# A hybrid decoder block on one core: substitution on 16x16 blocks, two copies of the merged inverses, and state updates through a PSUM bank of their own

## The chip, the cores and the metric

The kernel runs on one core of a Trainium2 chip. The metric is the time of one execution on the device in microseconds (us). Matrix products run on TensorE (PE; its weight loads are listed apart as PEld), elementwise work on VectorE (DVE), ScalarE (ACT) and GpSimd (POOL); DMAs are issued from the queues of SyncE (SP) and of ACT. Each engine takes its instructions in a fixed order and waits on semaphores for the others.

## What is computed

One decoder layer over 2048 tokens of width 1024: an RMS norm, one input projection of 3080 columns that feeds three mixers (a convolution module with 31 taps, a gated DeltaNet with 4 heads of 64, and differential attention with 4 heads), an output projection with the residual, and a SwiGLU feed-forward part of width 2816. All in float32. The change lies in the DeltaNet. Its core, per head and per chunk of c = 64 tokens:

```python
lower = jnp.where(strict, beta[..., None] * kk * decay, 0.0)
a_mat = lower + jnp.eye(c)
sol = lax.linalg.triangular_solve(a_mat, rhs, left_side=True, lower=True, unit_diagonal=True)
u_c, w_c = sol[..., :dv], sol[..., dv:]
def step(state, inp):                       # one chunk after the other
    v_new = u_i - w_i @ state
    o_i = (q_i * exp(g_i)) @ state + qk_i @ v_new
    state = state * exp(g_last) + (k_i * exp(g_last - g_i)).T @ v_new
```

## The kernel before

The 2048 tokens are worked on in four units (u = 0 to 3) of U = 512 tokens, which is 8 chunks of 64. With 4 heads a unit has 32 triangular systems of 64x64. A list of steps sets the order in which the program is written (line 937): for each unit N (first norm, `ln1`), I (`gdn_in`: the DeltaNet's part of the projection, with `gdn_gates`, `gdn_decays` and `gdn_conv`), G (`gdn_unit`), C (`conv_in` and `conv_taps`), L (`conv_ln`), K and V (queries, keys and values of attention). A scheduler then orders the instructions of each engine once, at build time; that order is fixed on the chip. After these steps come the rest of attention and the feed-forward part, from about 1000 us on.

The projection's matmuls are done by `mm3` (lines 137 to 139) in three products of a high and a low half; tiles `mz`, `mq`, `ma`, `mw`, `mg`, `mv` are its results in two PSUM banks that take turns, so a matmul into one waits for the eviction of the one before the last (for `ma` the DVE operation that makes `ql`). In unit 0 each weight tile is split into halves by ACT (line 120) and POOL (line 121, a tensor_tensor on 128x512 in SBUF), and written back to DRAM (`ws`); later units load both halves (`wp<-ws`) through SP's queue.

`gdn_unit` makes the matrix `L` (tokens of a chunk on partitions), writes it to DRAM (`gL`) and reads its two diagonal 32x32 blocks back as `Lg`, one system on each of 64 partitions. Lines 466 to 472 invert them: 31 steps, in each a product `tm` and a subtraction from `Tt`, each on DVE and each waiting for the one before. `Tt` and its transpose go out to `gT` and come back by ACT's DMA queue as `X64` (lines 480 to 482) and `T1` (line 483). Two groups of 32x32 matmuls (`yp` line 490, `wp` line 500, not to be mixed up with the weight tile `wp`) merge the two 32x32 inverses into the 64x64 inverse, and the result is put into `X64`. There is one `X64` for all units. Then the scan goes through the 8 chunks: `vp` (lines 542 and 545), its copy `vn` on ACT, `op` (550, 553), and `dp`, the product that updates the state (557); line 562 adds it to the state `Sbd`, one operation on 64x64 for each head.

`conv_taps` sums 31 taps for two halves of the channels on DVE (lines 586 to 593), with the sum in the PSUM tile `cp` until the last tap writes `ca` in SBUF.

Of the kernel before, what the change touches and what calls it, by code (L numbers as in the profile page):

```python
# [26 lines left out]
H = 4  # L27
# [20 lines left out]
def body(ctx: ExitStack, tc: tile.TileContext, x, norm1_g, w_in, conv_dw_w, conv_dw_b,  # L48
# [17 lines left out]
    gT = [dram.tile([2, 2, H, 8, 32, 32], F32, name=f"gT{u}", tag=f"gT{u}") for u in range(NU)]  # L66
# [6 lines left out]
    def cst(shape, name):  # L73
        return const.tile(shape, F32, name=name, tag=name)
# [115 lines left out]
    ps_ca = p1bctx.enter_context(tc.tile_pool(name="ps_ca", bufs=1, space=PSUM))  # L190
# [57 lines left out]
    X64 = cst([P, H, TU, C], "X64")  # L248
    V.memset(X64, 0.0)
# [8 lines left out]
    def sct_(name):  # L258
        return ps_sc.tile([P, 512], F32, name=name, tag="sc")
# [78 lines left out]
    def sm(u, name, n=16, bufs=1):  # L338
        return gd.tile([P, n], F32, name=f"{name}{u}", tag=name, bufs=bufs)
# [4 lines left out]
    def gdn_gates(u, abt):  # L344
# [12 lines left out]
        for c in (15, 13, 11, 9, 7, 5, 3):  # L357
# [14 lines left out]
        Gc, E1, Ek, EGL = sm(u, "Gc"), sm(u, "E1"), sm(u, "Ek"), sm(u, "EGL", 32, 2)  # L372
# [57 lines left out]
    def gdn_unit(u, qtok, sc):  # L430
        L, QKT = sc["L"], sc["QKT"]
# [25 lines left out]
        nc.scalar.dma_start(gL[u].rearrange("h (t p) c -> p (h t) c", p=P), L.rearrange("p h t c -> p (h t) c"))  # L457

        Lg = gd.tile([64, 32, 32], F32, name=f"Lg{u}", tag="Lg")
        Tt = gd.tile([64, 32, 32], F32, name=f"Tt{u}", tag="Tt")  # L460
        for blk in range(2):
            b0 = blk * 32
            nc.scalar.dma_start(Lg[b0:b0 + 32], gL[u].rearrange("h (c r) s -> (h c) r s", c=8)[:, b0:b0 + 32, b0:b0 + 32])
        V.memset(Tt, 0.0)
        V.memset(Tt.rearrange("p a b -> p (a b)")[:, 0:1024:33], 1.0)
        for j in range(31):
            n = 31 - j
            tm = gd.tile([64, 256], F32, name=f"tm{u}_{j}", tag="tg")
# [7 lines left out]
        T1 = gd.tile([P, H, TU, 32], F32, name=f"T1_{u}", tag="Lg")  # L476
        for ch in range(2):
            for blk in range(2):
                r0 = ch * C + blk * 32
                nc.scalar.dma_start(  # L480
                    X64[r0:r0 + 32, :, :, blk * 32:blk * 32 + 32].rearrange("p h t c -> p (h t) c"),
                    gT[u][1, blk].rearrange("h (t c) s q -> c s (h t) q", c=2)[ch])
            nc.scalar.dma_start(T1[ch * C:ch * C + 32].rearrange("p h t c -> p (h t) c"),
                              gT[u][0, 0].rearrange("h (t c) s q -> c s (h t) q", c=2)[ch])
# [98 lines left out]
    def conv_taps(u, hc):  # L583

        acc2 = gd.tile([P, 2, U], F32, name=f"ca{u}", tag="ca")
        for ct in range(2):
            acc = ps_ca.tile([P, U], F32, name=f"cp{u}_{ct}", tag="cp")
            for j in range(31):
                w, hj = cwT[:, ct, j:j + 1], hc[:, ct, j:j + U]
                if j == 0:  # L590
                    V.tensor_scalar(acc, hj, w, cwT[:, ct, 31:32], op0=ALU.mult, op1=ALU.add)
                else:
                    V.scalar_tensor_tensor(acc2[:, ct, :] if j == 30 else acc, hj, w, acc, op0=ALU.mult, op1=ALU.add)  # L593
        return acc2

    def conv_ln(u, acc2):
# [405 lines left out]
    hx = Rot([P, U], F32, (gd, "Tt"), (gd, "Lg"), (gd, "L"))  # L1002
# [261 lines left out]
```

## Time and profile before

| | us |
|---|---|
| median of 3 executions (2912.79 to 2918.99) | 2916.71 |
| the profiled execution | 2917.14 |
| its span, first to last instruction | 2915.4 |
| PE busy in the span | 2800.1 |
| DVE busy | 1565.9 |
| ACT busy | 1050.0 |
| POOL busy | 1111.3 |

Busy times are of the whole span, and the stages differ: the part before 1000 us holds all of the DeltaNet, the rest is attention and feed-forward. A busy time of PE counts overlapping matmuls once. Where a row names a wait, the number in brackets is the engine's idle time before the instruction, and the name behind the arrow is what ended it.

### The profile page before, as it was taken

Reading aid. Unit: us, or ns where it says so; the run is one execution under the profiler, and the core shown is the slowest. Engines: PE = TensorE matmul, PEld = TensorE weight load, DVE = VectorE, ACT = ScalarE, POOL = GpSimd, SP = SyncE. Lnnn points to the kernel's source line nnn. Section 1 sums busy time; section 2 is a strip of 40 time slices with the busy share of each in tenths; the row PEclk is TensorE's granted clock in tenths of the full one; section 3 lists DMA queues with packets and bytes.
Section 4 is the critical chain, followed back from the end, with each engine's and each line's share of the span. In section 5 each row is a group of like instructions: output and inputs, shape, how many; then the busy total and the mean of one; then the engine's idle time right before and its main releaser. Section 6 shows DMA issues by size and latency. Waiting matters only on the chain.

```text
span 2915.4 us, 39754 instructions
## 1 busy us (share of the span) xinstructions
PE 2800.1 (96%) x14673; PEld 2284.4 (78%) x14673; DVE 1565.9 (54%) x3443; ACT 1050.0 (36%) x2237; POOL 1111.3 (38%) x1021
## 2 busy tenths in 40 slices
PE   7979989999988999999998999999999999999998
PEld 6867777778776788887877888887878888888886
DVE  8976776877766765565566655541332222422223
ACT  4333223322154544444455434442332222322222
POOL 4421010001033444344455434444644444444543
PEclk9989999999988999999999999999999999999999
DMA  7784573654776544444366344324343333323332
GB/s 253 242 274 153 178 232 127 207 179 138 254 200 219 144 131 122 112 126 118 108 182 203 86 130 120 93 88 151 102 149 99 96 94 101 116 87 102 101 94 87
DMA packets 404064, 422.52 MB, mean 145 GB/s; under 512 B 46448, under 2 KB 326170, under 8 KB 392606
## 3 DMA queue, kind: packets, MB, share of 16 engines
q1 hardware_dynamic: 344222, 373.31, 41.8%
q10 hardware_dynamic: 59648, 46.67, 5.1%
q8 instruction: 116, 1.90, 0.3%
q14 instruction: 78, 0.64, 0.1%
HBM read 344.35 MB, written 75.56 MB: 144 GB/s over the span
## 4 chain that ended last, share of the span: by engine, by line
PE 80%; DVE 8%; DMA 6%; issue 2%; ACT 2%; POOL 1%; ACTq 0%; SPq 0%; POOLq 0%; DVEq 0%
PE pg L137 6%; PE pg L138 6%; PE pg L139 6%; PE pu L139 5%; PE pu L137 5%; PE pu L138 5%; PE pd L137 5%; PE pd L138 5%; PE pd L139 5%; PE s L784 3%; PE pt L830 2%; PE po L137 1%; PE po L138 1%; PE po L139 1%; PE ma L137 1%
## 5 line engine op out<-in xcount | busy, mean ns | idle before, releaser
L121 POOL TENSOR_TENSOR wp<-wr,wp 128x512 fp32r<-128x512 f32 (+1 forms) x666 | 906.7, 1386 | 865.4 <-ACT wp L120 847.9
L120 ACT CAST wp<-wr 128x512 fp32r<-128x512 f32 (+1 forms) x666 | 378.6, 617 | 871.5 <-PE pd L139 229.1
L137 PE MATMUL pd<-wp,ac 128*128 128x512 f32 x704 | 279.8, 400 | 9.2 <-DVE x L1154 7.6
L1154 DVE TENSOR_TENSOR x<-x,pd 128x512 f32<-128x512 f32 x192 | 130.4, 685 | 285.6 <-PE pd L139 285.2
L137 PE MATMUL pg<-h,wp 128*128 128x512 f32 x704 | 279.6, 397 | 3.4 <-ACT h L1075 1.7
L138 PE MATMUL pd<-wp,ac 128*128 128x512 f32 x704 | 277.1, 394 | 2.1 <-POOL wp L121 2.1
L139 PE MATMUL pd<-wp,ac 128*128 128x512 f32 x704 | 277.5, 394 | 1.5 <-DVE ac L1138 1.5
L139 PE MATMUL pu<-h,wp 128*128 128x512 f32 x704 | 278.4, 396 | 0.0
L139 PE MATMUL pg<-h,wp 128*128 128x512 f32 x704 | 278.3, 395 | 0.0
L137 PE MATMUL pu<-h,wp 128*128 128x512 f32 x704 | 277.3, 394 | 0.6 <-DVE ft L1135 0.6
L138 PE MATMUL pu<-h,wp 128*128 128x512 f32 x704 | 277.8, 395 | 0.0
L138 PE MATMUL pg<-h,wp 128*128 128x512 f32 x704 | 277.6, 394 | 0.0
L1134 DVE SCALAR_TENSOR_TENSOR ft<-ft,pg 128x512 f32<-128x512 f32 x88 | 60.4, 686 | 244.1 <-ACT ft L1133 244.1
L784 PE MATMUL s<-kk,qq 128*128 128x512 f32 (+3 forms) x576 | 171.6, 384 | 5.5 <-DVE mx L787 5.1
L593 DVE SCALAR_TENSOR_TENSOR cp<-hc,cwT,cp 128x512 f32<-128x512 f32 x232 | 173.2, 747 | 2.5
L137 PEld LDWEIGHTS pd<-wp,ac 128*128 128x128 f32 x704 | 132.7, 188 | 45.8 <-DVE x L1154 15.1
L137 PEld LDWEIGHTS pg<-h,wp 128*128 128x128 f32 x704 | 132.3, 188 | 36.2 <-ACT wp L120 5.4
L139 PEld LDWEIGHTS pd<-wp,ac 128*128 128x128 f32 x704 | 132.5, 188 | 31.7 <-DVE ac L1138 3.1
L138 PEld LDWEIGHTS pd<-wp,ac 128*128 128x128 f32 x704 | 132.8, 189 | 30.2 <-POOL wp L121 3.5
L137 PEld LDWEIGHTS pu<-h,wp 128*128 128x128 f32 x704 | 132.3, 188 | 30.0 <-ACT wp L120 1.0
L138 PEld LDWEIGHTS pu<-h,wp 128*128 128x128 f32 x704 | 132.3, 188 | 29.7
L138 PEld LDWEIGHTS pg<-h,wp 128*128 128x128 f32 x704 | 132.3, 188 | 28.8 <-DVE h L1076 0.2
(389 smaller groups left out, 5866.0 us busy)
## 6 DMA issues: line engine op xcount, KB each, us to landing
wr<-in_w_ffn_in_dram SPq DMA_DIRECT2D x176, 512.0 KB, 3.9
wp<-ws SPq DMA_DIRECT2D x66, 1024.0 KB, 5.8
wr<-in_w_ffn_out_dram SPq DMA_DIRECT2D x88, 512.0 KB, 3.5
ws<-wp SPq DMA_DIRECT2D x22, 1024.0 KB, 6.9
wr<-in_w_out_dram SPq DMA_DIRECT2D x44, 512.0 KB, 3.6
arena<-vs SPq DMA_DIRECT2D x80, 256.0 KB, 3.8
kk<-ks SPq DMA_DIRECT2D x64, 256.0 KB, 5.0
qq<-qs SPq DMA_DIRECT2D x96, 128.0 KB, 4.5
```

The lines of the kernel that those rows point to most:

```text
L120: A.copy(w[:, 0, q], raw[:, q])
L121: G.tensor_tensor(w[:, 1, q], raw[:, q], w[:, 0, q].bitcast(F32), op=ALU.subtract)
L137: T.matmul(ps, lhsT=lh, rhs=rh, start=start, stop=False)
L138: T.matmul(ps, lhsT=lh, rhs=rl, start=False, stop=False)
L139: T.matmul(ps, lhsT=ll, rhs=rh, start=False, stop=stop)
L593: V.scalar_tensor_tensor(acc2[:, ct, :] if j == 30 else acc, hj, w, acc, op0=ALU.mult, op1=ALU.add)
L784: T.matmul(sp[:, 0:w], lhsT=qq[c][:, l, q0:q0 + P], rhs=kt_[x][c][:, k0:k0 + w], start=l == 0, stop=l == 1)
L830: T.transpose(pt[:, col:col + P], ptile[b][kt // 8][:, (kt % 8) * P:(kt % 8 + 1) * P], ident)
L1134: V.scalar_tensor_tensor(t_, t_, 1.0, pg, op0=ALU.add, op1=ALU.mult)
L1154: V.tensor_tensor(xs_, xs_, pd, op=ALU.add)
```

## The change

The inversion by substitution is done on 16x16 blocks: four for each system, so one system's block on each of 128 partitions, in 15 steps. `gT` holds the inverses of the four blocks. A new merge stage in front of the old one makes the 32x32 inverses from pairs of 16x16 ones with matmuls: `zp` (64 matmuls of 32x32), copied by ACT, then `vm` (64) and `nm` (32). For that, the inverses are also loaded as `D16`, and the blocks of L beside the diagonal as `L16`, both through SP's queue; `X64` is loaded in 8 pieces rather than 4, `T1` is now computed on DVE and not loaded. There are two `X64` tiles, used in turn by the units.

In units 0 to 2 the state's update goes through one PSUM tile `dpz` of its own, whose cross blocks are set to zero once: four 64x64 matmuls for a chunk, and two DVE operations on 128x128 where there were four on 64x64. Unit 3 keeps the old form. The bank for `dpz` is the one in which `conv_taps` had its sum; the taps now add up in SBUF, in `ca` itself. The tile `ty` of `conv_ln` moves to a slot that `gdn_conv` uses too.

```diff
-    ps_ca = p1bctx.enter_context(tc.tile_pool(name="ps_ca", bufs=1, space=PSUM))
+    ps_dp = p1bctx.enter_context(tc.tile_pool(name="ps_dp", bufs=1, space=PSUM))
...
-    X64 = cst([P, H, TU, C], "X64")
-    V.memset(X64, 0.0)
+    dpz = ps_dp.tile([P, 2, P], F32, name="dpz", tag="dpz")
+    V.memset(dpz, 0.0)
+    XX = [gd.tile([P, H, TU, C], F32, name="X0", tag="X0"), cst([P, H, TU, C], "X1")]
+    for X64 in XX:
+        V.memset(X64, 0.0)
+    D16 = gd.tile([P, H, TU, 32], F32, name="D16", tag="D16")
+    V.memset(D16, 0.0)
+    L16 = gd.tile([P, H, TU, 32], F32, name="L16", tag="L16")
+    V.memset(L16, 0.0)
...
+        for ch in range(2):
+            for blk in range(2):
+                r0 = blk * 32
+                nc.sync.dma_start(
+                    L16[ch * C + r0 + 16:ch * C + r0 + 32, :, :, 0:16].rearrange("p h t c -> p (h t) c"),
+                    gL[u].rearrange("h (t c r) s -> c r (h t) s", c=2, r=C)[ch, r0 + 16:r0 + 32, :, r0:r0 + 16])
...
-        for j in range(31):
-            n = 31 - j
-            tm = gd.tile([64, 256], F32, name=f"tm{u}_{j}", tag="tg")
+        for j in range(15):
+            n = 15 - j
+            tm = gd.tile([P, 64], F32, name=f"tm{u}_{j}", tag="tg")
...
+            for k in range(4):
+                r0 = ch * C + k * 16
+                for dst, m, c0 in ((X64, 1, k * 16), (D16, 0, k % 2 * 16)):
+                    if m or k < 3:
+                        (nc.scalar if m else nc.sync).dma_start(
+                            dst[r0:r0 + 16, :, :, c0:c0 + 16].rearrange("p h t c -> p (h t) c"),
+                            gT[u][m, k].rearrange("h (t c) s q -> c s (h t) q", c=2)[ch])
+        zp = sct_(f"zp{u}")
+        for th in range(TU * H):
+            for r0 in range(0, P, 32):
+                T.matmul(zp[r0:r0 + 32, th * 32:th * 32 + 32], lhsT=L16[r0:r0 + 32, th % H, th // H, :],
+                         rhs=X64[r0:r0 + 32, th % H, th // H, r0 % C:r0 % C + 32], start=th == 0,
+                         stop=th == TU * H - 1, skip_group_check=True)
+        zs_ = gd.tile([P, TU * H, 32], F32, name=f"zm{u}", tag="dd")
+        A.copy(zs_, zp.rearrange("p (h x) -> p h x", x=32))
+        vp_ = sct_(f"vm{u}")
+        for th in range(TU * H):
+            for r0 in range(0, P, 32):
+                T.matmul(vp_[r0:r0 + 32, th * 32:th * 32 + 32], lhsT=D16[r0:r0 + 32, th % H, th // H, :],
+                         rhs=zs_[r0:r0 + 32, th, :], start=th == 0, stop=th == TU * H - 1, skip_group_check=True)
...
+        for r0 in (0, C):
+            V.tensor_tensor(T1[r0:r0 + 32].rearrange("p h t x -> p t h x"),
+                            D16[r0:r0 + 32].rearrange("p h t x -> p t h x"),
+                            np_[r0:r0 + 32, :].rearrange("p (t h x) -> p t h x", t=TU, h=H), op=ALU.subtract)
...
+                if u < NU - 1:
+                    for h in range(H):
+                        p, r0 = h // 2, h % 2 * C
+                        T.matmul(dpz[r0:r0 + C, p, r0:r0 + C], lhsT=kdv[cs, h, :], rhs=vn[cs, h * C:h * C + C],
+                                 start=True, stop=True, skip_group_check=True)
+                    for p in range(2):
+                        V.scalar_tensor_tensor(Sbd[:, p, :], Sbd[:, p, :], sc["EGL"][:, tt, p, ch:ch + 1], dpz[:, p, :],
+                                               op0=ALU.mult, op1=ALU.add)
+                    continue
...
-            acc = ps_ca.tile([P, U], F32, name=f"cp{u}_{ct}", tag="cp")
+            a = acc2[:, ct, :]
...
-                    V.scalar_tensor_tensor(acc2[:, ct, :] if j == 30 else acc, hj, w, acc, op0=ALU.mult, op1=ALU.add)
+                    V.scalar_tensor_tensor(a, hj, w, a, op0=ALU.mult, op1=ALU.add)
```

On DVE, around unit 0's inversion: the taps of the convolution (`cp`, in the changed kernel `ca`), the norm of the next unit (`ht`), the inversion (`tm`, `Tt`) and the evictions `ql`, which free the bank that PE waits for. Before:

```order
L593 SCALAR_TENSOR_TENSOR cp_1_1026<-hc_850,cwT,cp_1_1026 128x512
L472 TENSOR_TENSOR Tt_1152<-Tt_1152,tm_4_1169 64x27x5
L303 SCALAR_TENSOR_TENSOR ht_1_1914<-ntp_2_1_2004,g1T,ht_1_1914 128x128
L593 SCALAR_TENSOR_TENSOR cp_1_1026<-hc_850,cwT,cp_1_1026 128x512
L470 TENSOR_TENSOR tm_5_1172<-Lg_1151,Tt_1152 64x156
```

And now:

```order
L312 SCALAR_TENSOR_TENSOR ht_1_2050<-ntp_3_1_2174,g1T,ht_1_2050 128x128
L492 TENSOR_TENSOR Tt_1163<-Tt_1163,tm_1_1173 128x14x2
L768 SCALAR_TENSOR_TENSOR ql_1544_2_2302<-ma_1544_2_2267,qh_1544_2_2301 128x512
L490 TENSOR_TENSOR tm_2_1176<-Lg_1162,Tt_1163 128x39
L312 SCALAR_TENSOR_TENSOR ht_0_2049<-ntp_3_0_2161,g1T,ht_0_2049 128x128
```

The taps stood between the steps of the inversion; now all of them stand ahead of its first step, and so ahead of the third `ql`.

On PE, the new merge of unit 0 stands among the products `ma` for attention:

```order
L137 MATMUL ma_2056_2_2427<-ht_1_172,wp_2428 128x512
L516 MATMUL vm_1299<-zm_1297,D_163 32x32 x64
L521 MATMUL nm_1364<-D_163,zm_1297 32x32 x32
L138 MATMUL ma_2056_2_2427<-ht_1_172,wp_2428 128x512
L139 MATMUL ma_2056_2_2427<-ht_1_172,wp_2428 128x512
```

Before, the first small matmuls of unit 0 were those of `yp`, and they stood later, among the products `mz` of unit 1:

```order
L616 MATMUL ctq_1_2400<-ident,cxn_1_2398 128x128
L604 MATMUL ctp_2_2405<-ident,ca_993 128x128 x2
L490 MATMUL yp_1260<-X_157,L_477 32x32 x16
L137 MATMUL mz_1_2484<-wp_2447,ht_0_1913 128x264
L138 MATMUL mz_1_2484<-wp_2447,ht_0_1913 128x264
```

What moved: the small matmuls begin about four `ma` tiles' worth of matmuls earlier, and there are three more blocks of them.

On SP's queue, in the same stretch, now (`D` is `D16`, `wr` a weight tile, `ws` its split halves in DRAM):

```order
L118 DMA wr_9417<-in_w_out_dram 128x2x512
L124 DMA ws_2475<-wp_2468 128x2048
L501 DMA D_163<-gT_67 16x16x16 x6
L114 DMA wp_2583<-ws_301 128x2x792
L114 DMA wp_2585<-ws_310 128x2x792
```

Before, the loads of the weights followed directly:

```order
L118 DMA wr_8889<-in_w_out_dram 128x2x512
L124 DMA ws_2339<-wp_2332 128x2048
L114 DMA wp_2447<-ws_293 128x2x792
L114 DMA wp_2449<-ws_302 128x2x792
L114 DMA wp_2451<-ws_311 128x2x528
```

What moved: six loads that wait for `gT` now stand ahead of the weights of unit 1.

## Rows read from the trace of the kernel before

**Rows 1.** The page's busy times: us, share of the span, number of instructions.

```profile
PE 2800.1 (96%) x14673; PEld 2284.4 (78%) x14673; DVE 1565.9 (54%) x3443; ACT 1050.0 (36%) x2237; POOL 1111.3 (38%) x1021
```

**Rows 2.** Busy time of the engines by stretch: the stretch, its length, busy us and (instructions) of PE, PEld, DVE, ACT, POOL, then the clock granted to PE as a share of full speed, the DMA share and GB/s.

```profile
100.00:150.00 50.00, 50.00 (x357) 44.04 (x356) 43.92 (x84) 16.96 (x38) 16.80 (x15) 0.98 0.78 256
150.00:200.00 50.00, 34.53 (x141) 27.52 (x140) 47.02 (x117) 16.25 (x40) 15.44 (x14) 0.83 0.76 271
200.00:400.00 200.00, 193.02 (x1264) 151.88 (x1262) 142.06 (x348) 60.37 (x144) 19.53 (x22) 0.99 0.58 190
400.00:600.00 200.00, 190.61 (x1252) 154.51 (x1253) 149.52 (x371) 58.15 (x139) 16.72 (x19) 0.97 0.55 172
600.00:800.00 200.00, 196.96 (x1329) 158.92 (x1328) 150.32 (x387) 46.80 (x101) 21.97 (x22) 0.98 0.60 196
800.00:1000.00 200.00, 180.34 (x1157) 145.14 (x1157) 137.73 (x409) 101.08 (x262) 80.01 (x98) 0.89 0.71 199
1000.00:2916.00 1916.00, 1875.43 (x8800) 1536.89 (x8798) 810.14 (x1561) 708.04 (x1424) 889.93 (x786) 1.00 0.38 115
```

**Rows 3.** What PE waited for: us in total, times, longest.

```profile
PE ma L137 <- DVE ql L711: 13.7, 3, 8.2
...
PE yp L490 <- DMA X<-gT: 4.7, 3, 2.4
PE mq L137 <- DMA wp<-ws: 4.1, 1, 4.1
```

**Rows 4.** Instructions in order of time on PE (start, length): a block of the old merge between products of the projection, and a block of 64x64 matmuls of the scan that alternates between two halves of the columns.

```profile
651.36 0.40 PE L139 MATMUL mg<-ht,wp 128*128 128x512 f32 x1
651.69 2.11 PE L500 MATMUL wp<-ys,T 32*32 32x32 f32 x64
653.72 0.50 PE L137 MATMUL mg<-ht,wp 128*128 128x512 f32 x1
654.06 0.40 PE L138 MATMUL mg<-ht,wp 128*128 128x512 f32 x1
...
884.69 0.45 PE L522 MATMUL vp<-X,prg 64*64 64x64 f32 x8
885.07 0.33 PE L524 MATMUL vp<-ident,prg 128*128 128x128 f32 x1
```

**Rows 5.** The same view at one chunk of the scan in unit 0: `op`, `dp` and the product behind them; then DVE's update of the state.

```profile
264.58 0.68 PE L553 MATMUL op<-vn,Q 64*64 64x64 f32 x8
265.18 0.71 PE L557 MATMUL dp<-vn,kd 64*128 64x128 f32 x4
265.82 0.50 PE L138 MATMUL mq<-ht,wp 128*128 128x512 f32 x1
...
265.93 1.17 DVE L562 SCALAR_TENSOR_TENSOR Sbd<-Sbd,EGL,dp 64x64 f32<-64x64 f32 x4 [1.57 <-PE dp L557]
```

**Rows 6.** DVE's busy time in the operations on `tm` alone, by the stretches in which the inversions of units 0 and 1 lie: length, busy us (operations), clock, DMA share, GB/s.

```profile
150.00:200.00 50.00, 24.05 (x62) 0.83 0.76 271
360.00:425.00 65.00, 20.74 (x62) 0.95 0.64 212
```

**Rows 7.** All operations on one tile or line: count, length in ns (least, median, most), first and last start. The inversion; the taps, whose sum is in PSUM; a sum of the same form whose operands are all in SBUF.

```profile
L470 DVE TENSOR_TENSOR tm<-Lg,Tt x124: 172/355/812, 156.1 to 787.0; 64x31 f32<-64x31 f32 x8, 64x60 f32<-64x60 f32 x8, 64x87 f32<-64x87 f32 x8, 64x112 f32<-64x112 f32 x8
L593 DVE SCALAR_TENSOR_TENSOR cp<-hc,cwT,cp x232: 721/746/757, 101.5 to 784.8; 128x512 f32<-128x512 f32 x116
L330 DVE SCALAR_TENSOR_TENSOR cc<-ut,qwT,cc x72: 734/752/1852, 47.5 to 656.0; 128x512 f32<-128x512 f32 x72
```

**Rows 8.** DVE and POOL side by side in order of time: three sums in SBUF beside two of POOL's, and four taps with the sum in PSUM beside two of POOL's.

```profile
72.03 2.96 POOL L121 TENSOR_TENSOR wp<-wr,wp 128x512 fp32r<-128x512 f32 x2 [4.92 <-ACT wp L120]
72.20 4.12 DVE L330 SCALAR_TENSOR_TENSOR cc<-ut,qwT,cc 128x512 f32<-128x512 f32 x3
...
104.03 2.81 POOL L121 TENSOR_TENSOR wp<-wr,wp 128x512 fp32r<-128x512 f32 x2 [3.08 <-ACT wp L120]
104.38 3.12 DVE L593 SCALAR_TENSOR_TENSOR cp<-hc,cwT,cp 128x512 f32<-128x512 f32 x4
```

**Rows 9.** Groups by line from 98 to 172 us, where unit 0's taps lie: count, busy us, mean ns, idle time before.

```profile
L593 DVE SCALAR_TENSOR_TENSOR cp<-hc,cwT,cp 128x512 f32<-128x512 f32 x58 | 43.4, 748 | 0.9
L728 DVE TENSOR_TENSOR ve<-mw,ve 128x512 fp32r<-128x512 f32 x4 | 2.7, 687 | 2.3 <-DMA vs<-ve 2.0 <-ACT ve L727 0.3
...
L121 POOL TENSOR_TENSOR wp<-wr,wp 128x512 fp32r<-128x512 f32 x18 | 23.5, 1330 | 33.5 <-ACT wp L120 33.4
```

**Rows 10.** PE in order of time at its longest waits for DVE in units 0 and 1, and for a weight in unit 1.

```profile
169.68 0.77 PE L137 MATMUL ma<-ht,wp 128*128 128x512 f32 x1 [8.19 <-DVE ql L711]
...
401.11 0.58 PE L137 MATMUL mw<-wp,ht 128*128 128x256 f32 x1 [2.36 <-DVE ve L728]
...
432.66 0.47 PE L137 MATMUL mq<-ht,wp 128*128 128x512 f32 x1 [4.14 <-DMA wp<-ws]
```

**Rows 11.** DVE at the start: the clearing of tiles, and the first sum over x that follows it.

```profile
1.69 0.91 DVE L249 MEMSET X<- 128x1024 f32 x1 [0.16 <-issue]
...
4.66 0.69 DVE L277 CUSTOM_DVE_ANT_0 ht<-x 128x512 fp32r<-128x512 f32 x1
```

**Rows 12.** The end of unit 0's scan on PE, and ACT's queue when it issues the first loads of unit 1's inverses.

```profile
353.26 0.71 PE L557 MATMUL dp<-vn,kd 64*128 64x128 f32 x4
...
428.19 0.90 ACTq L480 DMA_DIRECT2D X<-gT  x2
```

More of the change, by code (lines that the diff above doesn't have):

```diff
@@ L65, in body @@
     gL = [dram.tile([H, U, C], F32, name=f"gL{u}", tag=f"gL{u}") for u in range(NU)]
-    gT = [dram.tile([2, 2, H, 8, 32, 32], F32, name=f"gT{u}", tag=f"gT{u}") for u in range(NU)]
+    gT = [dram.tile([2, 4, H, 8, 16, 16], F32, name=f"gT{u}", tag=f"gT{u}") for u in range(NU)]
     const = ctx.enter_context(tc.tile_pool(name="const", bufs=1))
@@ L376, in gdn_gates @@
         A.activation(Ek, Ek, AF.Exp)
-        A.activation(EGL, tp[:, 128:160], AF.Exp)
+        EGL = EGL.rearrange("p (t a c) -> p t a c", t=TU, c=2)
+        gl = tp[:, 128:160].rearrange("p (t a b c) -> p t a b c", t=TU, b=2, c=2)
+        for b in range(2):
+            A.activation(EGL[b * C:b * C + C], gl[b * C:b * C + C, :, :, b, :], AF.Exp)
         return dict(g=v3(g), be=v3(be), G=v3(Gc), E1=v3(E1), Ek=v3(Ek),
-                    EGL=EGL.rearrange("p (t h c) -> p t h c", h=H, c=2))
+                    EGL=EGL)
     def gdn_decays(u, sc):
@@ L430, in gdn_unit @@
     def gdn_unit(u, qtok, sc):
-        L, QKT = sc["L"], sc["QKT"]
+        L, QKT, X64 = sc["L"], sc["QKT"], XX[u % 2]
         def qkh(tt):
@@ L475, in gdn_unit @@
         nc.scalar.dma_start(gT[u][1].rearrange("k h c a b -> (k h c) a b"), Lg)
-        T1 = gd.tile([P, H, TU, 32], F32, name=f"T1_{u}", tag="Lg")
         for ch in range(2):
[L478 to L484, printed above, removed]
+            for k in range(4):
+                r0 = ch * C + k * 16
[4 more added lines that the diff above has]
+                            gT[u][m, k].rearrange("h (t c) s q -> c s (h t) q", c=2)[ch])
@@ new lines, in gdn_unit @@
+        vp_ = sct_(f"vm{u}")
[3 more added lines that the diff above has]
+                         rhs=zs_[r0:r0 + 32, th, :], start=th == 0, stop=th == TU * H - 1, skip_group_check=True)
+        np_ = ps_sc.tile([P, 512], F32, name=f"nm{u}", tag="o")
+        for th in range(TU * H):
+            for r0 in (0, C):
+                T.matmul(np_[r0:r0 + 32, th * 32:th * 32 + 32], lhsT=zs_[r0:r0 + 32, th, :],
+                         rhs=D16[r0:r0 + 32, th % H, th // H, :], start=th == 0, stop=th == TU * H - 1,
+                         skip_group_check=True)
@@ new lines, in gdn_unit @@
+        T1 = p1.tile([P, H, TU, 32], F32, name=f"T1_{u}", tag="pr")
+        for r0 in range(0, P, 32):
+            A.mul(X64[r0:r0 + 16, :, :, r0 % C + 16:r0 % C + 32].rearrange("p h t x -> p t h x"),
+                  vp_[r0:r0 + 16, :].rearrange("p (t h x) -> p t h x", t=TU, h=H)[:, :, :, 16:32], -1.0)
+        for r0 in (0, C):
+            V.tensor_tensor(T1[r0:r0 + 32].rearrange("p h t x -> p t h x"),
+                            D16[r0:r0 + 32].rearrange("p h t x -> p t h x"),
+                            np_[r0:r0 + 32, :].rearrange("p (t h x) -> p t h x", t=TU, h=H), op=ALU.subtract)
@@ L590, in conv_taps @@
                 if j == 0:
-                    V.tensor_scalar(acc, hj, w, cwT[:, ct, 31:32], op0=ALU.mult, op1=ALU.add)
+                    V.tensor_scalar(a, hj, w, cwT[:, ct, 31:32], op0=ALU.mult, op1=ALU.add)
                 else:
-                    V.scalar_tensor_tensor(acc2[:, ct, :] if j == 30 else acc, hj, w, acc, op0=ALU.mult, op1=ALU.add)
+                    V.scalar_tensor_tensor(a, hj, w, a, op0=ALU.mult, op1=ALU.add)
         return acc2
@@ L620, in conv_ln @@
             yl = acc2[:, ct, :]
-            ty = gd.tile([P, U], F32, name=f"cy{u}_{ct}", tag="cm", bufs=CMB)
+            ty = p1.tile([P, U], F32, name=f"cy{u}_{ct}", tag="cc")
             A.activation(ty, yl, AF.Tanh)
@@ L1001, in body @@
     hy = [q0[:, k] for k in range(3)] + [gd.tile([P, 2, U], F32R, name="hy3", tag="QKT", bufs=2)]
-    hx = Rot([P, U], F32, (gd, "Tt"), (gd, "Lg"), (gd, "L"))
+    hx = Rot([P, U], F32, (gd, "X0"), (gd, "hc"), (gd, "L"))
     hyr = Rot([P, U], F32, (gd, "dd"), (gd, "tg"))
```

20 lines of the change are left out of this document (10 added, 10 removed).

## The prediction

> **What bounds the kernel now.** I read the busy times first: PE works in 2800.1 of 2915.4 us, DVE in 1565.9 [rows 1]. An average over the whole span hides stages, so the table by stretch comes next [rows 2]. Past 1000 us PE works 1875.4 of 1916 us, and nothing of this change is left there. From 200 to 800 us PE works 580.6 of 600, while DVE has a quarter of its time free: what PE gets to do more costs time there, and what DVE is spared does not, save where PE waits for it. Two stretches differ. From 150 to 200 us PE works 34.5 of 50 us at a clock of 0.83 and DVE 47.0: DVE is the bound. From 800 to 1000 us PE has some 20 us idle at a clock of 0.89, but that is where unit 3's scan runs beside the start of attention, and unit 3 keeps the old state update.
>
> The list of PE's waits says who is late [rows 3]: `ma` for DVE's `ql`, 13.7 us in three waits; the small matmuls `yp` for the loads of `X`, 4.7; a weight from the queue, 4.1. The longest single one is 8.19 us, at 169.7 us [rows 10]. PE takes it because DVE, in its fixed order, is at taps and at steps of the inversion.
>
> **The sum is made against the profiled execution**, 2917.1 us, which is 0.4 above the median of the three; its span is 2915.4.
>
> *Small matmuls of the new merge.* Each float32 matmul of the program is two passes in the trace: `wp` has 32 and shows 64, which begin at 651.69 and end where the next product begins, 653.72, so 31.7 ns for a pass [rows 4]. `zp`, `vm` and `nm` add 64 + 64 + 32 = 160 matmuls, 320 passes a unit. One after the other that is 10.1 us a unit, 40.6 in all. But `wp` stays in one block of the array for 16 matmuls; the new ones change it with each. What that gives is shown only for two halves of the columns: eight 64x64 passes that alternate take 0.38 us with the switch behind them (884.69 to 885.07), eight in one half 0.60 (264.58 to 265.18) [rows 4, 5]. Two at once would make 20.3 us. `zp` and `vm` go through four blocks that share neither rows nor columns; if four run at once they take 256 x 7.9 ns = 2.0 us a unit and `nm`, with two blocks, 1.0: 12.2 us in all. No row shows four. I take the middle of these two, **+16** (12 to 41): a pair loses hardly anything in the row, and four is more of the same.
>
> The Trainium skill speaks against that (TensorEngine Tiling (Array Packing), "Restrictions and Gotchas"): it says that different row tiles cannot access the same PSUM bank at once, and all of `zp` is one bank. In the row that runs pairs both have the same rows, so it does not test this. By the rule this term would be 40.6.
>
> *Switches of shape.* The block of `wp` costs 0.1 us in front and 0.1 behind (651.36 to 651.69 and 653.72 to 654.06, where 0.23 is the pace of the products) [rows 4]. Three more blocks in four units, and some nine single `zp` that the order puts alone: **+4**.
>
> *State updates.* `dp` holds PE for 0.64 us a chunk (265.18 to 265.82) [rows 5]. Four 64x64 matmuls that alternate between two halves are the eight passes of 0.38, and they follow `op` in its own shape, which saves a switch: some 0.3 saved in 24 chunks, **-7** (-6 to -10). On DVE four operations of 1.17 us become two [rows 5]; that ends the chain of a chunk sooner, but the order has several us of products between `dp` and the next `vp`, so it is worth nothing in time.
>
> *Start.* DVE clears a second `X` (0.91 us [rows 11]) and two tiles of half its size more, and a smaller `Tt`; the first sum over x stands behind that, and PE waits for it: **+1**.
>
> *DVE in unit 0.* The inversion takes DVE 24.05 us [rows 6]. Now it is 30 operations on 15 to 64 elements; 31 elements take 172 ns and the median one 355 [rows 7], so about 0.19 each, 6 us: 18 spared, and 1.5 at clearing and copying `Tt`. Against it: `T1`, two operations of the 0.69 us that 512 elements from PSUM take [rows 9], and the taps. A tap with its sum in PSUM takes 0.75 us whatever POOL does [rows 7, 8]. A sum with all operands in SBUF takes 0.75 alone, but three of them beside two operations of POOL took 4.12 us instead of 2.3: each operation of POOL holds one up by 0.9 [rows 8]. Under unit 0's taps lie 18 operations of POOL [rows 9]; if each holds up one tap that is +16. So DVE's work up to 200 us stays about as it is, 18 + 1.5 spared and 16 + 1.4 added. The taps now stand first, so the first two `ql` come later and the last ones at the old time: **0** (-15 to +8). In units 1 to 3 POOL is nearly idle under the taps.
>
> *DVE in units 1 to 3.* 14 us less for each inversion [rows 6], where PE is the bound. What it can give back is PE's waits for DVE: 2.36 us at 401 and shorter ones around it [rows 10], with the clock at 0.95 in this stretch, which costs as much again [rows 6]: **-6** (0 to -12).
>
> *New waits.* A unit's inverses now come in 14 loads of 256 pieces and the blocks of L in 4 more, 4608 pieces of 64 bytes instead of 3072 of 128. The waits that hang on this traffic are `yp` for `X`, 4.7 us, and a weight, 4.1 [rows 3, 10]. `zp` takes over the wait of `yp`; the traffic is half as much again: **+3** (-3 to +12). ACT copies `zp` (0.6 us) and scales four pieces; the order puts 2 to 5 us of products between these stages, which hide it.
>
> *The second X64.* Unit 1's loads of `X` begin at 428.2 us, 75 us after the last `dp` of unit 0, at 353.3 [rows 12]. No load waited for the old tile, so this part does nothing, in every case here.
>
> Sum: 16 + 4 - 7 + 1 + 0 - 6 + 3 = +11, so **2928 us**.
>
> **The rivals.**
> 1. *Unit 0 sets PE free: faster.* If POOL holds up fewer than half of the taps that I count, because POOL's operations fall beside DVE work that reads PSUM, 9 us or more of DVE's relief is left, the 12.2 us of `ma`'s two long waits go, and the clock there is no longer 0.83 [rows 2, 10]: -15 instead of 0. With four matmuls at once (12), -9 in units 1 to 3 and +1 of waits: 12 + 4 - 7 + 1 - 15 - 9 + 1 = -13, **2904**. It decides from about ten taps held up. For it: DVE has 6 us free from 100 to 150 us, where most of these taps lie. Against it: the row with three sums, where each operation of POOL hit one.
> 2. *It cancels.* Four at once, no new waits, and a little more from units 1 to 3: 12 + 4 - 7 + 1 - 9 = +1, **2918**.
> 3. *One small matmul at a time.* 40.6 instead of 16: **2952**. The whole of it counts, since PE is full where these blocks stand. The Trainium skill's rule above would bring this about.
> 4. *SP's queue.* The loads of `D16` wait for `gT` in front of the next weights. If in each unit PE then waits for a weight as long as in the row, 4.14 us, that is +16: **2944**. Against it: three weight tiles are held ahead, 15 us of products.
>
> **How the numbers follow.** Forecast 0.36, the first rival 0.25, the second 0.17, the third 0.12, the fourth 0.10. A measurement of this kernel tells about 0.2% from no change, so 2911 to 2923 counts as the same. Of the first rival 0.23 is faster, and a little of the second: 0.25. The second, and the ends of the forecast and of the first, give 0.24 of same; the rest is slower, 0.51. The forecast's own terms reach some 10 us either way; the range runs from a little beyond the first rival to just below the third, **2902 to 2950**, and leaves a tenth out on each side.
>
> **What the profile after would show.** `zp` and `vm` at 8 to 16 ns a pass (the term stands), or at 32 (rival 3). Taps of unit 0 at 1.6 us beside POOL and 0.75 elsewhere, some 18 of them; few would mean rival 1, with PE's stretch from 150 to 200 us fuller than 34.5. The operations on `tm` at about 6 us a unit. The four matmuls of `dpz` at 0.3 us. Waits of `zp` for `X`, `D` or `L`, and of weights, at about 12 us together. PE's busy time past 1000 us unchanged. I would be wrong above all if PE's waits before 1000 us move as a whole, since the new order shifts every matmul up to there.

## The result, and the profile after

| | us |
|---|---|
| kernel before, median of 4 executions (2912.79 to 2919.34) | 2917.85 |
| changed kernel, median of 4 (2944.45 to 2953.37) | 2947.99 |
| ratio, with its 95% interval | 1.0109 (1.0094 to 1.0123) |
| the profiled execution after, and its span | 2946.48, 2944.8 |

The change makes the kernel 30 us slower: inside the range of 2902 to 2950, on the side that the forecast gave, but nearly three times the 11 us that its sum came to.

The first view is again the table by stretch (engine columns as in [rows 2]), now of the changed kernel.

```profile
25.00:100.00 75.00, 68.91 (x336) 56.12 (x334) 66.78 (x122) 32.55 (x69) 37.49 (x28) 0.95 0.73 246
100.00:150.00 50.00, 41.73 (x314) 37.55 (x314) 48.98 (x73) 13.34 (x27) 19.99 (x14) 0.97 0.59 196
150.00:200.00 50.00, 35.55 (x146) 27.18 (x144) 41.11 (x95) 18.97 (x50) 19.04 (x16) 0.90 0.89 291
...
600.00:800.00 200.00, 190.78 (x1628) 153.76 (x1628) 121.31 (x326) 52.44 (x117) 18.72 (x22) 0.97 0.55 178
800.00:1000.00 200.00, 178.60 (x1465) 144.93 (x1464) 127.86 (x382) 85.13 (x227) 60.91 (x78) 0.89 0.69 203
1000.00:2945.00 1945.00, 1903.82 (x8947) 1563.91 (x8945) 827.09 (x1613) 725.39 (x1467) 908.00 (x806) 0.99 0.39 116
```

From 100 to 150 us DVE has gone from 43.92 us busy to 48.98, which is full, and PE from 50.00 to 41.73 [rows 2]. From 600 to 800 DVE is busy for 29 us less, and PE, which is the bound there, gains nothing by it. From 100 to 200 us together DVE is as busy as before (90.1 us for 90.9), but more of its work lies in the first half, and PE works 77.3 us of the 100 where it worked 84.5.

The list of PE's waits (columns as in [rows 3]):

```profile
PE ma L137 <- DVE ql L768: 12.2, 6, 3.6
...
PE ma L137 <- DVE ql L765: 8.7, 4, 3.7
...
PE zp L508 <- DMA X<-gT: 5.2, 5, 3.0
PE ctq L673 <- DVE cxn L670: 4.9, 2, 4.2
...
PE kt L457 <- DVE pr L450: 4.3, 3, 2.0
PE mq L137 <- DMA wp<-ws: 4.2, 1, 4.2
PE kk L465 <- DVE Q L469: 4.1, 2, 2.1
```

`ma` still waits for `ql`, 20.9 us in all where it was 13.7 [rows 3], but only 8.9 of them lie in unit 0, where all of the 13.7 lay; the other 12 are new and stand behind it. New in unit 0 are waits for other DVE operations: `kt` for `pr` and `kk` for `Q` (transposes and products on the way to `L`), 8.4 us between 101 and 139 us, beside the taps, and 4.2 of the 4.9 of `ctq`. `zp` has taken over the wait of `yp` (5.2 for 4.7), and the weight is as late as before.

**PE's time by tile.** If each matmul is charged with the time from its start to the next one's, as far as PE was busy, PE's time splits as follows (worked out from all matmuls of both traces, us):

| | before | after |
|---|---|---|
| `zp`, `vm`, `nm` | 0 | 17.9 |
| `dp` and `dpz` | 21.2 | 10.8 |
| `op` | 40.9 | 37.2 |
| `ma` and `mw` (the same instructions) | 291.7 | 303.4 |
| all other matmuls | 2446.3 | 2440.7 |
| idle | 98.1 | 116.6 |

The work that the change adds and removes comes to +3.8. The rest is 18.5 us more idle time and some 6 us in which the same matmuls ran longer, at a lower clock (0.979 granted over the execution, before 0.982).

**Where it was lost.** A time in one trace can't be set against the same time in another, since the order differs. But all the matmuls that the two kernels share can be added up in their order, each at its pace in the trace of before, and the times at which the two have done the same amount can be compared. By this measure the changed kernel is 2.5 us late at 100 us of the kernel before, loses 13.3 between 100 and 270 (unit 0), 8.0 between 270 and 750 (units 1 and 2, and most of unit 3's projection) and 6.3 between 750 and 1650 (the end of unit 3 beside the start of attention), and nothing later. The table behind the experiments gives this for each of them.

### The profile page after: what moved, and what is told of

Read it like the earlier page. It is cut to its first block, busy times and chain, and to the rows that moved or that the text cites. A ratio compares the mean times of both kernels' runs of the same rounds, so it can differ in the third digit from the quotient of the medians.

```text
span 2944.8 us, 42464 instructions
## 1 busy us (share of the span) xinstructions
PE 2810.0 (95%) x16049; PEld 2296.0 (78%) x16049; DVE 1504.5 (51%) x3279; ACT 1057.8 (36%) x2261; POOL 1114.9 (38%) x1021
## 4 chain that ended last, share of the span: by engine, by line
PE 78%; DMA 9%; DVE 8%; issue 2%; ACT 2%; POOL 1%; SPq 1%; ACTq 0%; POOLq 0%; DVEq 0%
PE pg L137 6%; PE pg L138 5%; PE pg L139 5%; PE pu L139 5%; PE pu L138 5%; PE pu L137 5%; PE pd L137 5%; PE pd L138 5%; PE pd L139 5%; PE s L841 3%; DVE ca L650 2%; PE pt L887 2%; PE po L139 1%; PE po L138 1%; PE po L137 1%
## 5 line engine op out<-in xcount | busy, mean ns | idle before, releaser
L650 DVE SCALAR_TENSOR_TENSOR ca<-hc,cwT,ca 128x512 f32<-128x512 f32 x240 | 190.4, 815 | 1.2
L137 PEld LDWEIGHTS pd<-wp,ac 128*128 128x128 f32 x704 | 132.6, 188 | 43.5 <-DVE x L1211 14.4
L137 PEld LDWEIGHTS pg<-h,wp 128*128 128x128 f32 x704 | 132.3, 188 | 36.4 <-ACT wp L120 6.0
L138 PEld LDWEIGHTS pu<-h,wp 128*128 128x128 f32 x704 | 132.3, 188 | 29.8
L138 PEld LDWEIGHTS pg<-h,wp 128*128 128x128 f32 x704 | 132.3, 188 | 29.2 <-DVE h L1133 0.2
L139 PEld LDWEIGHTS pg<-h,wp 128*128 128x128 f32 x704 | 132.3, 188 | 29.1
```

Of the source, the lines that this page charges most:

```text
L137: T.matmul(ps, lhsT=lh, rhs=rh, start=start, stop=False)
L138: T.matmul(ps, lhsT=lh, rhs=rl, start=False, stop=False)
L139: T.matmul(ps, lhsT=ll, rhs=rh, start=False, stop=stop)
L650: V.scalar_tensor_tensor(a, hj, w, a, op0=ALU.mult, op1=ALU.add)
```

## The experiments

Theory A: the taps of unit 0, now summed in SBUF, are held up by POOL, and PE loses there. Rival B: the new merge stage, with its waits, is the loss. Rival C: the scheduler's new order is. All ratios are to the kernel before on the same chip, whose medians there were 2917.6 to 2919.2 (single executions 2905.7 to 2930.3).

**1. The taps in SBUF alone**

```diff
-            acc = ps_ca.tile([P, U], F32, name=f"cp{u}_{ct}", tag="cp")
+            a = acc2[:, ct, :]
...
-                    V.scalar_tensor_tensor(acc2[:, ct, :] if j == 30 else acc, hj, w, acc, op0=ALU.mult, op1=ALU.add)
+                    V.scalar_tensor_tensor(a, hj, w, a, op0=ALU.mult, op1=ALU.add)
```

> The kernel before, with one edit: the taps add up in SBUF instead of PSUM; the inversion, the merge and the state update are the old ones. Theory A (taps): the taps of unit 0 are held up by POOL's splits of weights, DVE has 14 us more to do there, and nothing shortens the inversion, so PE waits longer between 100 and 235 us: +14 to +22 us on the kernel before. Rival B (merge): the loss of the change comes from the new merge stage, its small loads and its waits; then this kernel is within 4 us of the kernel before. Rival C (order): any edit makes the scheduler put the instructions in another order, which alone moves the time by some 10 us either way; then this kernel moves without longer taps beside POOL.

Measured: 2939.2 us, 1.0066 (1.0041 to 1.0091): +20. Theory A's size; but in the table by stage below, 9.7 of it are lost in unit 0 and 17.6 behind 750 us, where theory A has nothing.

**2. The blocks without the state part** (the changed kernel, taps in PSUM and old updates in all units)

```diff
-    ps_dp = p1bctx.enter_context(tc.tile_pool(name="ps_dp", bufs=1, space=PSUM))
+    ps_ca = p1bctx.enter_context(tc.tile_pool(name="ps_ca", bufs=1, space=PSUM))
...
-                if u < NU - 1:
-                    for h in range(H):
...
-                    V.scalar_tensor_tensor(a, hj, w, a, op0=ALU.mult, op1=ALU.add)
+                    V.scalar_tensor_tensor(acc2[:, ct, :] if j == 30 else acc, hj, w, acc, op0=ALU.mult, op1=ALU.add)
```

> The changed kernel with its state part taken back: 16x16 blocks, new merge stage and two X64 stay; taps add up in PSUM, and the state update is the old product with four operations. Theory A: the small matmuls and switches (+17), waits (+3) against DVE's relief in unit 0 (-12) and after it (-6): 0 to +8 us on the kernel before. Rival B: the merge and its waits cost the 30 us by themselves, and the state part gains some 10: +25 to +40.

Measured: 2952.2, 1.0107 (1.0082 to 1.0131): +33. Rival B's size: without the taps' loss, the blocks cost as much as the whole change. Theory A alone falls, and the two losses don't add up: 20 and 33, less what the state updates give, would be 43.

**3. The state part alone** (updates in their own bank, taps in SBUF, old inversion and merge)

```diff
+    dpz = ps_dp.tile([P, 2, P], F32, name="dpz", tag="dpz")
+    V.memset(dpz, 0.0)
...
+                if u < NU - 1:
+                    for h in range(H):
+                        p, r0 = h // 2, h % 2 * C
+                        T.matmul(dpz[r0:r0 + C, p, r0:r0 + C], lhsT=kdv[cs, h, :], rhs=vn[cs, h * C:h * C + C],
+                                 start=True, stop=True, skip_group_check=True)
```

> The kernel before with the state part alone: state updates through the bank of their own in units 0 to 2, taps in SBUF, old inversion and merge. Theory A: as with the taps alone, less 7 to 10 us for the state updates: +6 to +14 us on the kernel before. Rival B: only the gain of the state updates is left, -7 to -10.

Measured: 2929.4, 1.0031 (1.0019 to 1.0044): +10, which is 10 less than the taps alone, as expected.

**4. The changed kernel with unit 0's taps in PSUM**

```diff
+            b = dpb.tile([P, U], F32, name=f"cp{u}_{ct}", tag="dpz") if u == 0 else a
...
-                    V.scalar_tensor_tensor(a, hj, w, a, op0=ALU.mult, op1=ALU.add)
+                    V.scalar_tensor_tensor(a if j == 30 else b, hj, w, b, op0=ALU.mult, op1=ALU.add)
+        if u == 0:
+            DZ.append(dpb.tile([P, 2, P], F32, name="dpz", tag="dpz"))
+            V.memset(DZ[0], 0.0)
```

> The changed kernel with one edit: the taps of unit 0 add up in the bank that the state updates use later (they are done with it before unit 0's first update), and the bank is cleared behind them; the taps of units 1 to 3 stay in SBUF. Theory A: taps of unit 0 at 0.75 us again, and the 19 to 21 us that PE lost there come back: -18 to -28 us on the changed kernel, so 2920 to 2930 us. Rival B: within 5 us of the changed kernel.

Measured: 2945.5 (2936.0 to 2953.6), 1.0081 (1.0054 to 1.0108). By the median only 2.5 us come back, which is rival B's size; by the profiled execution (2936.0), the fastest of five, 10.5. The intervals of this kernel and of the changed one overlap. In the profiled execution the stage itself does what theory A says. These are the groups by line from 98 to 178 us (count, busy us, mean ns, idle before), first of the changed kernel, then of this one:

```profile
L650 DVE SCALAR_TENSOR_TENSOR ca<-hc,cwT,ca 128x512 f32<-128x512 f32 x60 | 58.0, 991 | 0.4
...
L121 POOL TENSOR_TENSOR wp<-wr,wp 128x512 fp32r<-128x512 f32 x20 | 31.1, 1579 | 38.4 <-ACT wp L120 38.4
```

```profile
L650 DVE SCALAR_TENSOR_TENSOR cp<-hc,cwT,cp 128x512 f32<-128x512 f32 x58 | 43.6, 751 | 1.0
...
L121 POOL TENSOR_TENSOR wp<-wr,wp 128x512 fp32r<-128x512 f32 x20 | 25.6, 1299 | 44.5 <-ACT wp L120 44.3
```

991 ns for a tap against 751: 14.4 us in 60 taps, 0.72 for each of POOL's 20 operations, which are longer themselves (1579 against 1299). At 260 us of equal work the changed kernel is 16.0 late and this one 0.9: what the taps lose in unit 0, PE loses in full there. But 10.6 is lost between 270 and 750 us, and 7.7 after that, as in experiment 2. So there is a second loss, and the next three runs look for it.

**5. The inversion cut short** (the kernel before)

```diff
-        for j in range(31):
+        for j in range(13):
```

> The kernel before with its inversion stopped after 13 of 31 steps (36 operations of DVE left out in each unit, about 16 us; the rest of the inverse is not computed). Nothing is put in its place: it shows what shorter work on DVE gives by itself. Theory A, the prediction's: unit 0's waits of PE for DVE go (-12 to -15) and a part of those in units 1 to 3 (-6): -15 to -21 us. Rival D (order and chains): PE's waits are not made by DVE being full but by where the evictions stand in the fixed order and by the copies and loads in the chain; then the time moves by less than 6 us.

Measured: 2932.1, 1.0046 (1.0032 to 1.0060): +14, outside both expectations, with 12 to 15 us less work for DVE in each unit. The prediction's claim that unit 0's waits go with DVE's relief finds no support. Up to 750 us the profiled execution is 7.8 us ahead, 4.3 by the end of unit 0 and 3.5 more by 750. Then it loses 17 between 750 and 1650, where the output projection `po` waits for its input:

```profile
PE po L137 <- ACT yt L1086: 11.7, 2, 8.0
PE ma L137 <- DVE ql L711: 10.3, 3, 6.9
```

And why only 4 in unit 0: one row of before shows that PE's long wait [rows 10] ends with DVE's `ql` at 168.86 us, and that most of the inversion stands behind it (51 of its 62 operations; the 13 steps kept here include all that stand ahead, so the run took nothing away there):

```profile
168.86 0.67 DVE L711 SCALAR_TENSOR_TENSOR ql<-ma,qh 128x512 fp32r<-128x512 f32 x1
...
174.12 0.38 DVE L470 TENSOR_TENSOR tm<-Lg,Tt 64x220 f32<-64x220 f32 x1
```

In experiment 4, which has the short inversion and fast taps, that wait is still there, since the same taps and evictions stand ahead of it; its inversion is over at 180.2 us and not at 199.1, which PE was not waiting for. PE and then DVE in order of time (the wait ends with `ql`; the view names the small operation that DVE does beside it):

```profile
173.51 0.77 PE L137 MATMUL ma<-ht,wp 128*128 128x512 f32 x1 [7.74 <-DVE nss L290]
...
172.69 0.68 DVE L771 SCALAR_TENSOR_TENSOR ql<-ma,qh 128x512 fp32r<-128x512 f32 x1
...
180.22 0.39 DVE L492 COPY Lg<-Tt 128x256 f32<-128x256 f32 x1
```

**6. The changed kernel without the merge stage**

```diff
-        zp = sct_(f"zp{u}")
-        for th in range(TU * H):
...
-            V.tensor_tensor(T1[r0:r0 + 32].rearrange("p h t x -> p t h x"),
-                            D16[r0:r0 + 32].rearrange("p h t x -> p t h x"),
-                            np_[r0:r0 + 32, :].rearrange("p (t h x) -> p t h x", t=TU, h=H), op=ALU.subtract)
+            V.tensor_copy(T1[r0:r0 + 32].rearrange("p h t x -> p t h x"),
+                          D16[r0:r0 + 32].rearrange("p h t x -> p t h x"))
```

> The changed kernel without the new merge stage: the matmuls zp, vm and nm, ACT's copy and its four scalings are left out, T1 is a copy of D16; all loads, the short inversion and the state part stay. Theory B' (the merge is what costs): the 18 us that these matmuls hold PE, and the 8 us that PE waits for their input and copy, go, while yp gets a wait of some 5 back: -18 to -26 us on the changed kernel, 2922 to 2930. Theory A (the taps cost most): -10 or less, since PE waits for DVE in unit 0 all the same.

Measured: 2935.8, 1.0062 (1.0039 to 1.0085), 12 less than the changed kernel: between the two expectations, and with an interval that reaches both. Unit 0 keeps its loss (13.1 where the changed kernel has 13.3), since PE waits for the taps there all the same; between 270 and 750 us 14.7 come back with the merge, 8.0 lost turned into 6.7 gained.

**7. The small matmuls block by block** (the changed kernel)

```diff
-        for th in range(TU * H):
-            for r0 in range(0, P, 32):
+        for r0 in range(0, P, 32):
+            for th in range(TU * H):
```

> The changed kernel with zp, vm and nm written block by block (all 16 matmuls of one 32x32 block of the array, then the next block), the same matmuls otherwise. If blocks that share neither rows nor columns run at once, as the trace shows (7 ns a pass), this takes that away: each pass 32 ns, 40 instead of 18 us in four units, so +20 to +25 us on the changed kernel. If the short passes have another cause, the time and the passes stay as they are.

Measured: 3000.7, 1.0290 (1.0262 to 1.0319), 53 more than the changed kernel. PE in order of time in unit 1, first of the changed kernel, then of this one:

```profile
426.43 0.38 PE L661 MATMUL ctp<-ident,ca 128*128 128x128 f32 x2
426.74 1.24 PE L508 MATMUL zp<-X,L 32*32 32x32 f32 x122
427.91 0.33 PE L673 MATMUL ctq<-ident,cxn 128*128 128x128 f32 x1
```

```profile
440.54 0.28 PE L139 MATMUL mw<-wp,ht 128*128 128x256 f32 x1
440.75 3.84 PE L516 MATMUL vm<-zm,D 32*32 32x32 f32 x125
444.40 0.21 PE L521 MATMUL nm<-D,zm 32*32 32x32 f32 x1
```

122 passes in 1.17 us (426.74 to 427.91) are 9.6 ns each; 125 in 3.65 (440.75 to 444.40) are 29.2. So passes in different blocks do overlap. The three products hold PE for 46.2 us in place of 17.9, 28 more where 20 to 25 were expected; the other 25 were not expected (see the last section).

**8. The state part with unit 0's taps in PSUM** (experiment 3 with the edit of experiment 4)

> The kernel before with the state updates through the bank of their own, and the taps of unit 0 adding up in that bank before the updates use it; taps of units 1 to 3 in SBUF, old inversion and merge. Theory A: the loss of the taps in unit 0 (19 us) is gone and the 10 us of the state updates are left: -6 to -12 us on the kernel before, faster than both kernels. Rival: taps in SBUF cost elsewhere too, or the new order costs as much as the updates give: within 4 us of the kernel before.

Measured: 2928.7 (2914.3 to 2935.3), 1.0034 (1.0018 to 1.0050): +11, outside both expectations, and level with experiment 3 (2929.4), from which it differs in unit 0's taps alone. Its profiled execution, 2914.3, is the fastest of 12; it is 8.5 us ahead at 750 us, the gain of the updates, and loses 6.6 of that by 1650.

**9 and 10. The order alone** (the kernel before with another priority of the DeltaNet's steps)

```diff
-    GP = 500
+    GP = 600
```

and 400 in the second.

> The kernel before with one number changed: the scheduler's priority of the DeltaNet's steps is 600 instead of 500. Every instruction is the same; only their order changes, on PE from about unit 1 on. Rival C (order): the kernel before stands in an order that its numbers were chosen for, and another one loses 5 to 17 us between 750 and 1050 us, as each of the edited kernels did, the one with less work among them. Against it: within 3 us of the kernel before, and the loss between 750 and 1050 us has to be put down to what each edit does.

> The same with 400: the order of PE changes from unit 3 on only, beside the start of attention. Rival C: again 5 to 17 us, all of it after 750 us. Against it: within 3 us of the kernel before.

Measured: 2919.9, 1.0007 (0.9988 to 1.0027), and 2915.3, 0.9988 (0.9975 to 1.0000). Both lie within 3 us, so rival C in its general form falls: another order does not cost 5 us by itself.

**11 and 12. The order of two changed kernels** (the changed kernel with 600; experiment 8 with 400; the edit as above)

> The changed kernel with the priority of the DeltaNet's steps at 600 instead of 500: the same instructions; the order of PE changes from about unit 2 on. Between 750 and 1050 us of work the profiles of all edited kernels show 6 to 18 us more idle time of PE than the kernel before. If that comes of the order, another order moves the changed kernel by 5 us or more (either way), with idle time of PE in that stretch moving as much; if it comes of the merge and the loads themselves, the time and the idle time stay within 4 us.

> The kernel before with the state updates in a bank of their own and unit 0's taps in that bank, and the priority at 400: the order of PE changes from unit 3 on only. By its profile that kernel was 8 us ahead of the kernel before at 750 us and lost that beside the start of attention. If the loss there is the order's, another order keeps a part of the 8 us: 2908 to 2916. If it stays, 2922 to 2932.

Measured: 2968.2, 1.0172 (1.0155 to 1.0188), 20 us more than the changed kernel with every instruction the same; and 2919.2, 1.0010 (0.9991 to 1.0028), between its two expectations and 10 less than experiment 8 by the medians, though the two intervals overlap. So order alone moves the changed kernel by 20 us; for the other pair it is not clear. Not as expected: in the profiles, the two orders of the changed kernel are level at 550 us of equal work and 15 us apart at 800, at a lower clock (0.92 against 0.96) and with 6 us more idle time of PE; and in the last kernel the stretch after 750 us is no better. No version here is clearly faster than the kernel before; the last one equals it.

**All of them by stage.** Differences from the kernel before at equal work of PE, in us, from one profiled execution each; "idle" is PE's idle time in the stretch from 750 to 1050. Where the first 270 us have nearly the same order (experiment 10), the second column differs by 7 at equal idle time and a clock of 0.89 against 0.93, so single numbers are uncertain by about that. Nor is each profiled execution a typical one: those of experiments 4 and 8 are 10 and 14 us below their medians, that of experiment 10 is 12 above.

| | to 100 | 100-270 | 270-750 | 750-1650 | idle |
|---|---|---|---|---|---|
| before | | | | | 19.7 |
| the change | 2.5 | 13.3 | 8.0 | 6.3 | 30.5 |
| 1 taps in SBUF | -0.1 | 9.7 | -3.6 | 17.6 | 25.9 |
| 2 blocks alone | 2.2 | 2.2 | 13.3 | 11.9 | 29.1 |
| 3 state part | -0.4 | 12.0 | -4.5 | 5.7 | 34.1 |
| 4 change, unit 0's taps in PSUM | 1.3 | 0.1 | 10.6 | 7.7 | 37.2 |
| 5 short inversion | -0.8 | -3.5 | -3.5 | 16.7 | 30.2 |
| 6 no merge | 2.3 | 13.1 | -6.7 | 10.7 | 35.1 |
| 7 block by block | 2.1 | 26.9 | 22.7 | 32.8 | 38.4 |
| 8 state, unit 0's taps in PSUM | -1.5 | 1.6 | -8.6 | 6.6 | 35.5 |
| 9 order, 600 | -1.4 | 4.9 | -7.7 | 4.5 | 23.0 |
| 10 order, 400 | -0.3 | 7.0 | -2.3 | 12.1 | 23.8 |
| 11 change, 600 | 3.3 | 16.3 | 19.0 | 6.1 | 37.7 |
| 12 state, 400 | -0.4 | 3.3 | -14.3 | 9.6 | 34.0 |

## Why the prediction was right in its sign and short in its size

**Small matmuls, +16: right, 17.9.** Passes of four blocks start 9.6 ns apart, experiment 7 shows that it is their taking turns among the blocks, and in the profile of experiment 6 PE gets the time back without them where it is full. Rival 3 falls. The Trainium skill's rule against it (TensorEngine Tiling (Array Packing), "Restrictions and Gotchas": different row tiles cannot access one PSUM bank at once) is not borne out here: the four row tiles of `zp` write one bank, each its own partitions, at 9.6 ns a pass, against 29.2 for one tile after the other. The +4 for switches of shape is not to be seen apart from these 17.9.

**State updates, -7: right in kind, too small.** `dp` and `dpz` take 10.4 less and `op`, which now runs into them, 3.7 less; experiments 1 and 3 are 10 apart. In the trace after, the updates' passes start among the last of `op` and the next of `vp`, so they cost less than eight passes by themselves:

```profile
264.34 0.22 PE L600 MATMUL op<-vn,Q 64*64 64x64 f32 x1
264.40 0.22 PE L605 MATMUL dpz<-vn,kd 64*64 64x64 f32 x1
264.40 0.22 PE L600 MATMUL op<-vn,Q 64*64 64x64 f32 x1
264.46 0.22 PE L605 MATMUL dpz<-vn,kd 64*64 64x64 f32 x1
264.46 0.22 PE L600 MATMUL op<-vn,Q 64*64 64x64 f32 x1
264.51 0.22 PE L605 MATMUL dpz<-vn,kd 64*64 64x64 f32 x2
264.52 0.27 PE L569 MATMUL vp<-X,prg 64*64 64x64 f32 x2
```

**DVE in unit 0, 0: this is the step that failed.** Both of its sides were sized well and one was put in the wrong place. The taps lost 14.4 us (16 forecast), each operation of POOL holding up 0.72 us (0.9 forecast). The Trainium skill names the cause (SBUF — State Buffer, "SBUF: two separate sides"): a DVE operation with two inputs in SBUF and a GpSimd operation that reads SBUF exclude each other for a whole instruction. The trace agrees, with both engines' operations longer, and with the sum in PSUM neither is. The inversion did shrink to what was said, in the same view as [rows 6]:

```profile
100.00:230.00 130.00, 6.15 (x30) 0.92 0.71 230
230.00:420.00 190.00, 6.01 (x30) 0.98 0.55 181
```

But the text called the two equal because DVE's work "up to 200 us" stays as it is, and let the last `ql` come at the old time. The taps stand ahead of the DVE operations that PE waits for in unit 0 (`pr`, `Q`, `ql`; for the first two 8.4 us, in experiment 4 2.0), and the bulk of the inversion behind them (experiment 5); in the changed kernel all of it stands behind the first two `ql`. So all eight `ql` of unit 0 come late, the first at 164.6 us for 154.5 and the last at 232.4 for 212.1; in experiment 4 these are 155.9 and 217.1. In the profiled executions the taps' 14.4 came through nearly in full (13.3 lost in unit 0, in experiment 4 0.1), and the 18 spared gave about 4, which is less than the 7 by which such a number can be off: some +10, not 0. That the whole time carries this loss is not shown: by the medians, experiments 4 and 8, which take it away, are only 2.5 and 0.7 us below the changed kernel and experiment 3. Busy time was added up over a stretch in which the order decides. Rivals 1 and 2, which wanted taps that POOL spares or a relief that counts, fall with it.

**DVE in units 1 to 3, -6: not shown.** Experiment 5 has -3.5 there, less than the uncertainty, and the changed kernel's idle time of PE there grew (below).

**New waits, +3: within its bounds.** `zp` waits 5.2 for its loads where `yp` waited 4.7: +0.5. PE also stands idle for 2.8 us within two blocks of `nm`, and no wait that the profile shows ends that. Weights are no later, so rival 4 falls. **Start, +1:** PE's first matmul comes 1.2 us later; 2.5 are lost by 100 us. **The second X64** was not tried alone.

**The whole.** Work on PE was forecast at 16 + 4 - 7 = +13 and came to 3.8. Waits, with the clock behind them, were forecast at 1 + 0 - 6 + 3 = -2 and came to 18.5 idle and 6 of clock. So the term that was mis-sized is PE's waiting. Of its 18.5 us, 0.4 lie before 100 us, 7.6 in unit 0 (26.7 for 19.1), 5.6 between 270 and 750, and 10.8 between 750 and 1050, of which 5.9 come back by 1650. For the last two the sum had next to nothing: it took the waits there to be those of before, less a little. The prediction named this as the way in which it would be wrong above all, that the new order moves PE's waits before 1000 us as a whole, but gave it no term. That the time still lies within the range, 2 us below its upper end, is luck as far as the mechanism goes: the ends were set from rivals 1 and 3, and both fell.

**What stays open.** Every kernel whose instructions were edited idles 6 to 19 us more than the kernel before between 750 and 1050 us, even the one with only work removed; the two with the order alone changed idle 3 to 4 more. Experiment 11 shows that order alone can be worth 20 us, so it may be that the numbers which set it were chosen for the kernel before. That is argued and not shown: no run gave an edited kernel the order of the kernel before.

## What to carry to other kernels

Work taken from an engine comes back only if it stood ahead of something that was waited for: look in the order of time at what lies between the wait's start and the instruction that ends it, rather than at busy shares. Before moving a sum from PSUM to SBUF, see what POOL does beside it. And where a scheduler orders the whole program, an edit also buys a new order, worth in one pair here as much as the edit's largest term: try the order's numbers again before judging the edit.

## What the runs showed of the hardware

Not expected: 32x32 matmuls in one block of the array, one after the other, cost nearly as much outside them as in them. In experiment 7 they take 28 us more than side by side; the program's other matmuls run 22 us longer, charged as above, and PE is idle for 3.6 more. In experiment 7 the busy times by stretch (engine columns as in [rows 2]) around `vm` and `nm` of unit 1 are

```profile
435.00:441.00 6.00, 6.00 (x103) 5.69 (x102) 1.91 (x5) 1.53 (x3) 0.89 (x2) 1.00 0.25 83
441.00:447.00 6.00, 6.00 (x191) 5.94 (x189) 0.54 (x1) 1.50 (x4) 0.00 (x0) 0.89 0.08 27
447.00:455.00 8.00, 8.00 (x85) 7.71 (x86) 4.92 (x10) 5.07 (x14) 1.32 (x2) 0.50 0.64 189
```

PE is never idle in these 20 us, and yet its clock falls to half, 1.2 GHz, for the products that follow, for 13.7 us in all. In the changed kernel it also falls behind unit 1's small matmuls, for 10.2 us, but there PE has been idle in front, 1.75 us of it within `nm`:

```profile
430.00:436.00 6.00, 4.25 (x209) 3.96 (x208) 1.33 (x2) 2.97 (x7) 0.00 (x0) 1.00 0.26 92
436.00:446.00 10.00, 10.00 (x97) 9.47 (x96) 2.61 (x7) 5.01 (x13) 0.33 (x1) 0.50 0.43 118
```

In unit 0 the two differ more: the changed kernel has a clock of 1.00 from 220 to 236 us, behind the same matmuls, and experiment 7 has 0.70 from 224 to 232 and 0.66 from 232 to 240. Over the execution the granted clock is 0.969, and 0.979 in the changed kernel: 0.031 of 2998.9 us is 93 us of full speed withheld, 0.021 of 2944.8 is 62. The 31 us between them are enough for the 22 by which the other matmuls run longer. That the small matmuls are what brings the clock down is argued from this one pair of kernels and not shown by itself.
